# A two-layer backbone on one core: TensorE's attention instructions pinned to written order, transposes and values two steps behind the scores

## The chip, the cores and the metric

The kernel runs on one NeuronCore of a Trainium2 chip. The metric is the device time of one execution in microseconds (us). The core's engines work side by side, each through a queue of its own that it takes in order: TensorE (PE) does matrix products and writes them to PSUM, VectorE (DVE) and ScalarE (ACT) do elementwise work and empty PSUM, GpSimd (POOL) does a few small vector operations, and SyncE (SP) issues the transfers from memory (DMA).

## The reference, cut to what matters

Two streams of 256 tokens ("lat" and "ctx", 1024 features) go through two layers: attention and a feed-forward block, then a state-space mixer and a feed-forward block. The change lies in layer 0's attention alone:

```
q, k, v = split(u @ w_in)                 # 16 query heads, 4 key/value heads of 64
qr, kr  = rope(q_lat), rope(k_lat)        # rotated in the lat stream
s_win   = qr . kr * scale, masked to |i - j| <= 128
s_ctx   = q . k_ctx * scale
p       = softmax([s_win, s_ctx, sink])
y_lat   = (p_win @ v_lat + p_ctx @ v_ctx) @ w_out
# ctx queries attend to ctx keys alone
m       = silu(c) @ w_mod[i] + b_mod[i]   # six modulation vectors of each layer
```

All is float32. Large products split each operand in a high part that TensorE multiplies as fp32r and a low part (the rest), and add three products: high by high, low by high, high by low.

## The kernel before

A framework builds the program. The kernel's author writes Python that emits instructions; tiles come from pools with a number of buffers for each tag; a list scheduler then orders every engine's instructions by its own model of when operands are ready. So the order on TensorE is not the order in the text, unless an instruction is pinned behind its predecessor.

Attention works in 8 **pairs** p of query heads and 3 **steps** t of each pair. Steps 0 and 1 are the two blocks of 128 lat queries (512 keys), step 2 is both blocks of ctx queries (256 keys each). A step goes through these stages:

- `scores(p, t)`: TensorE writes two PSUM banks `s` (one for each head, a = 0 and 1), in fp32r with 128x128 weights, with a bf16 product for the mask in steps 0 and 1. VectorE takes the maxima (two reductions), three small operations make the bias, ScalarE takes the exponentials into `P` (two for each step, four in step 2) and one for the sink, VectorE adds, inverts and scales `P`.
- `mix(p, t)`: eight float32 transposes `pt` of 128x128 (TensorE), two copies to `PT` (ScalarE), then the values `o`: float32 products with 64 columns of weights, the two heads in the two column halves of the array. In steps 0 and 1 that is 8 instructions of 128 columns, in step 2 it is 4 of 256. ScalarE and VectorE split the sum into `oh` and `ol`.
- `q_gemm(p)`: 24 fp32r products of 512 columns for one pair's queries (`q`), copied to `qf`; `q_parts(p)` splits and rotates them (VectorE and ScalarE) into `qe`, `qo`, `re`, `ro`. `emit_w` splits every weight tile into `wh` (ScalarE) and `wl` (VectorE).
- the **filler**: `mods` computes three blocks of layer 0's modulation, each of 8 loads `wm` of 512 KB and 4 float32 products for each (`mod`, 32 columns of weights, the four in the four column quarters), then two transposes and two additions.

The text of `attention` runs the mix of a step one step behind its scores, a query product after the scores of t = 1, and one filler piece a step (two at t = 1). `kv_start` runs before attention, the output product `ao` behind it. PSUM has 8 banks: 4 of tag `mm` (scores, q), 3 of `aux` (pt, o), one `md` (mod). SP's queue holds the loads of `wm` (two buffers) and of raw weights `raw` (two buffers), in order.

In the profile a matrix instruction of float32 stands as two records, one of fp32r, bf16 or of a transpose as one.

Of the kernel before, what the change touches and what calls it, by code (L numbers as in the profile page):

```python
# [39 lines left out]
class Net:  # L40
# [33 lines left out]

    def gemm(self, ps, w, ah, al, c0, c1, ks=range(8)):
        mm = self.nc.tensor.matmul
# [13 lines left out]
    def mods_mm(self, ps, k, wm):  # L90
        n = wm.shape[1] // 4
        for j in range(4):
            self.nc.tensor.matmul(ps[32 * j:32 * j + 32, 0:n], self.cs[:, k, :], wm[:, j * n:(j + 1) * n],
                                  start=(k == 0), stop=(k == 7))

    def mods_out(self, i, ps, n, cuts, streams=(0, 1)):

        nc = self.nc
        m4 = self.tmp.tile([128, 256], F32, tag="t1", name="m4")[:, :n]
        nc.scalar.copy(m4, ps[:, 0:n])  # L100
        q = n // 128
        pt = ps[:, 256:512]
        for c in range(q):
            nc.tensor.transpose(pt[:, c * 128:(c + 1) * 128], m4[:, c * 128:(c + 1) * 128], self.ident)
# [58 lines left out]
    def run(self, gen):  # L163
        for _ in gen:
            pass

# [277 lines left out]
    def scores(self, p, t, q):  # L444
        nc = self.nc
        mm = nc.tensor.matmul
        qe, qo, re, ro = q
        g = p // 2
        P = [self.ap.tile([128, 512], F32, tag="P", name=f"P{p}{t}{a}", bufs=4) for a in range(2)]
# [43 lines left out]
    def mix(self, p, t, P):  # L493
        nc = self.nc
        g = p // 2
        PT = [self.ap.tile([128, 512], F32, tag="PT", name=f"PT{p}{t}{a}", bufs=3) for a in range(2)]
        for a in range(2):
            pt = self.bank("aux", f"pt{p}{t}{a}")
            for c in range(4):

                o = c if t < 2 else 2 * (c % 2) + c // 2
                nc.tensor.transpose(pt[:, o * 128:o * 128 + 128], P[a][:, c * 128:c * 128 + 128], self.ident)
            nc.scalar.copy(PT[a], pt)
        n, keys = (128, range(4)) if t < 2 else (256, range(2, 4))
        po = self.bank("aux", f"o{p}{t}")[:, :n]
        for i, kt in enumerate(keys):
            for a in range(2):
                nc.tensor.matmul(po[64 * a:64 * a + 64, :], self.V[:, kt, g * 64:g * 64 + 64],  # L508
                                 PT[a][:, i * n:i * n + n], start=(i == 0), stop=(i == len(keys) - 1))
# [26 lines left out]
    def kv_start(self, uh, ul):  # L536
# [17 lines left out]
        self.qs = {}  # L554
        for h in range(4):
# [4 lines left out]
            for t in range(4):  # L560
# [4 lines left out]
                if h == 3 and t == 1:  # L565
                    self.qs[0] = self.q_parts(0, q0)
# [15 lines left out]
    def attention(self, uh, ul, filler, k0, kr, k1, q1):  # L582
        qs = self.qs
        pend = []
        for p in range(8):
            q = qs.pop(p)
            for t in range(3):
                P = self.scores(p, t, q)
                pend.append((p, t, P))
                if p == 0 and t == 0:  # L590
                    qf = self.q_gemm(2, uh, ul, "aux")
                    self.k_parts(1, k0, kr)
                    kr = self.k_rope(k1)
                    qs[1] = self.q_parts(1, q1)
                if p == 0 and t == 1:
# [12 lines left out]

    def q_gemm(self, p, uh, ul, tag):
        w = self.next_w()  # L610
        ps = self.bank(tag, f"q{p}")
        self.gemm(ps, w, uh, ul, 0, 512)
        qf = self.ap.tile([128, 512], F32, tag="qf", name=f"qf{p}", bufs=1)
        self.nc.scalar.copy(qf, ps)
        return qf

    def q_parts(self, p, ps):
        qe = self.aq.tile([128, 512], F32R, tag="qe", name=f"qe{p}", bufs=3)
        qo = self.aq.tile([128, 512], F32R, tag="qo", name=f"qo{p}", bufs=3)
        re = self.aq.tile([128, 256], F32R, tag="re", name=f"re{p}", bufs=3)  # L620
        ro = self.aq.tile([128, 256], F32R, tag="ro", name=f"ro{p}", bufs=3)
        self.qsplit(qe, qo, ps)
        qr = self.aq.tile([128, 256], F32, tag="kr", name=f"qr{p}")
        self.rope(qr, ps[:, 0:256])
        self.qsplit(re, ro, qr)
        return qe, qo, re, ro


    def setup(self, ctx):
        tc, nc, a = self.tc, self.nc, self.a  # L630
        self.ctx = ctx
        pool = lambda n, b, **k: ctx.enter_context(tc.tile_pool(name=n, bufs=b, **k))
# [541 lines left out]
```

## Time and profile before

| | us |
|---|---|
| median of 3 runs (lowest to highest) | 1193.76 (1191.71 to 1194.17) |
| the profiled execution | 1194.7 |
| its span in the trace | 1192.9 |
| TensorE busy | 1140.3 (96%) |
| VectorE busy | 839.5 (70%) |
| ScalarE busy | 604.3 (51%) |
| DMA, mean over the span | 153 GB/s |

1.8 us of the profiled execution lie outside its span. A busy TensorE is an engine that has an instruction in flight; the ends of its instructions are modelled and overlap, so what its instructions cost is read from start to start. Positions below are us from the start of the span. Attention takes from 64.3 (the first product of pair 2's queries) to 220.5 (the last product of the values).

### The profile page before, as it was taken

What the parts mean: (1) busy time and instruction counts of PE and PEld (TensorE: products, weight loads), DVE (VectorE), ACT (ScalarE), POOL (GpSimd) and SP (SyncE); (2) the same over time, 40 slices, a digit from 0 to 9 for tenths busy, and PEclk for the clock granted to TensorE, in tenths of its full rate; (3) what the DMA queues carried; (4) which work ended last, traced back from release to release, by engine and by line L of the source; (5) the groups of instructions that cost most, each with busy time, mean ns of one, the idle gap of its engine ahead of it and who ended that gap; (6) DMA issues with size and microseconds to landing.
All of it is one profiled execution on the core that took longest, in us unless ns stands there. A gap on an engine that the chain in (4) does not pass through costs nothing.

```text
span 1192.9 us, 18539 instructions
## 1 busy us (share of the span) xinstructions
PE 1140.3 (96%) x6976; PEld 917.5 (77%) x6976; DVE 839.5 (70%) x1701; ACT 604.3 (51%) x1382; POOL 48.1 (4%) x79
## 2 busy tenths in 40 slices
PE   5999999998999999999999999999999996999996
PEld 4766666887987878887898777777777575898895
DVE  4498677677967677763434879889898769565566
ACT  4376566325532322321422737687868857454551
POOL 1200000003100000000000310000000000000000
PEclk8999999999999999999999989999999998999999
DMA  8834322342445466762222124443545572555551
GB/s 323 305 106 156 128 85 94 91 157 72 159 160 182 157 226 207 249 215 92 85 71 87 64 107 128 131 153 129 189 142 155 186 242 83 200 177 182 202 181 71
DMA packets 41433, 182.79 MB, mean 153 GB/s; under 512 B 4608, under 2 KB 5248, under 8 KB 28288
## 3 DMA queue, kind: packets, MB, share of 16 engines
q1 hardware_dynamic: 41056, 181.36, 45.1%
q8 instruction: 55, 0.90, 0.3%
q10 hardware_dynamic: 288, 0.26, 0.1%
q14 instruction: 34, 0.28, 0.1%
HBM read 180.41 MB, written 1.18 MB: 152 GB/s over the span
## 4 chain that ended last, share of the span: by engine, by line
PE 79%; DVE 8%; DMA 5%; ACT 5%; issue 1%; DVEq 0%; SPq 0%; ACTq 0%
PE f0a L79 5%; PE f0a L80 5%; PE f0a L81 5%; PE f0b L79 5%; PE f0b L81 5%; PE f0b L80 5%; PE y L947 3%; PE o L508 2%; PE f L265 2%; PE f L264 2%; PE f L263 2%; PE f1a L81 2%; PE f1a L79 2%; PE f1a L80 2%; DMA raw<-in_wall 2%; PE x L81 2%
## 5 line engine op out<-in xcount | busy, mean ns | idle before, releaser
L61 ACT CAST wh<-raw 128x512 fp32r<-128x512 f32 x404 | 237.6, 619 | 400.5 <-PE f0b L80 126.3
L62 DVE TENSOR_TENSOR wl<-raw,wh 128x512 fp32r<-128x512 f32 x404 | 268.4, 686 | 129.3 <-ACT wh L61 128.4
L79 PE MATMUL f0b<-f0fh,wh 128*128 128x512 f32 (+1 forms) x320 | 113.8, 356 | 0.0
L79 PE MATMUL f0a<-u1h,wh 128*128 128x512 f32 (+1 forms) x320 | 112.2, 353 | 1.5 <-ACT u1h L183 1.5
L81 PE MATMUL f0b<-f0fh,wl 128*128 128x512 f32 (+1 forms) x320 | 111.9, 350 | 0.0
L80 PE MATMUL f0a<-u1l,wh 128*128 128x512 f32 (+1 forms) x320 | 111.4, 350 | 0.0
L81 PE MATMUL f0a<-u1h,wl 128*128 128x512 f32 (+1 forms) x320 | 111.4, 349 | 0.0
L80 PE MATMUL f0b<-f0fl,wh 128*128 128x512 f32 (+1 forms) x320 | 111.1, 347 | 0.1
L142 DVE SCALAR_TENSOR_TENSOR ma<-wm,cs,ma 128x1024 f32<-128x1024 f32 x70 | 88.7, 1280 | 17.8 <-DMA wm<-in_w_mod 17.7
L79 PEld LDWEIGHTS f0a<-u1h,wh 128*128 128x128 f32 x320 | 61.1, 192 | 11.8 <-ACT u1h L183 2.3
L81 PEld LDWEIGHTS f0b<-f0fh,wl 128*128 128x128 f32 x320 | 60.1, 188 | 10.4 <-issue 2.1
L79 PEld LDWEIGHTS f0b<-f0fh,wh 128*128 128x128 f32 x320 | 60.1, 188 | 10.4 <-issue 2.6
L80 PEld LDWEIGHTS f0b<-f0fl,wh 128*128 128x128 f32 x320 | 60.2, 188 | 9.7 <-issue 1.4
L81 PEld LDWEIGHTS f0a<-u1h,wl 128*128 128x128 f32 x320 | 61.2, 191 | 8.0 <-issue 0.4
L80 PEld LDWEIGHTS f0a<-u1l,wh 128*128 128x128 f32 x320 | 61.0, 191 | 7.7 <-issue 0.4
L79 PE MATMUL f1a<-u4h,wh 128*128 128x256 f32 x224 | 63.5, 284 | 0.0
L81 PE MATMUL f1a<-u4h,wl 128*128 128x256 f32 x224 | 63.5, 283 | 0.0
L80 PE MATMUL f1a<-u4l,wh 128*128 128x256 f32 x224 | 63.4, 283 | 0.0
L79 PE MATMUL x<-u2h,wh 128*128 128x512 f32 x128 | 51.5, 402 | 2.2 <-DVE cy L758 2.2
L931 ACT ACTIVATE W<-A,sT 128x128 f32<-128x128 f32 (+1 forms) x128 | 50.0, 458 | 3.8 <-PE y L947 2.5
L351 DVE SCALAR_TENSOR_TENSOR X<-f0b,mT,X 128x256 f32<-128x256 f32 x48 | 21.0, 478 | 44.0 <-PE f0b L81 44.0
L81 PE MATMUL x<-u2h,wl 128*128 128x512 f32 x128 | 51.3, 402 | 0.3 <-DVE wl L62 0.3
(439 smaller groups left out, 2747.3 us busy)
## 6 DMA issues: line engine op xcount, KB each, us to landing
raw<-in_wall SPq DMA_DIRECT2D x102, 1024.0 KB, 5.0
wm<-in_w_mod SPq DMA_DIRECT2D x96, 512.0 KB, 4.3
A<-dq SPq DMA_DIRECT2D x32, 256.0 KB, 4.7
E<-dq SPq DMA_DIRECT2D x32, 256.0 KB, 5.0
X<-in_xT SPq DMA_DIRECT2D x8, 256.0 KB, 8.1
gate<-in_rows SPq DMA_DIRECT2D x2, 512.0 KB, 12.9
out_dram<-Xt SPq DMA_DIRECT2D x4, 256.0 KB, 2.0
mixg<-in_rows SPq DMA_DIRECT2D x1, 512.0 KB, 6.1
```

The costliest lines, as they stand in the source:

```text
L61: nc.scalar.copy(h, src[:, c])
L62: nc.vector.tensor_sub(l, src[:, c], h.bitcast(F32))
L79: mm(ps, wh[:, k, :], ah[k][:, c0:c1], start=(k == 0), stop=False)
L80: mm(ps, wh[:, k, :], al[k][:, c0:c1], start=False, stop=False)
L81: mm(ps, wl[:, k, :], ah[k][:, c0:c1], start=False, stop=(k == 7))
L142: nc.vector.scalar_tensor_tensor(t, wm, c, t, op0=ALU.mult, op1=ALU.add)
L263: mm(ps, lh(i), wh[:, c], start=(k == 0), stop=False)
L264: mm(ps, ll(i), wh[:, c], start=False, stop=False)
L265: mm(ps, lh(i), wl[:, c], start=False, stop=last)
L508: nc.tensor.matmul(po[64 * a:64 * a + 64, :], self.V[:, kt, g * 64:g * 64 + 64], PT[a][:, i * n:i * n + n], start=(i == 0), stop=(i == len ...
L931: nc.scalar.activation(W[:, h, o:o + l1 - l0], A[:, h, l0:l1], AF.Relu, scale=-1.0, bias=self.sT[:, st, r + h:r + h + 1])
L947: mm(ps[64 * a:64 * a + 64, l0:l1], lh[:, hc:hc + 64], mv, start=(n == 0), stop=(n == 5))
```

## The change

`pin(True)` makes `self.mm` and `self.tr` wrap every TensorE product and transpose traced in attention, the filler's and the query products' too, in `keep_in_program_order`: an edge of order behind the instruction written before on TensorE. The other engines and SP stay with the scheduler. `mix` is cut into `turn` (transposes and copies) and `mix` (values). One step now writes, in this order: the transposes of the step two behind, the scores of its own, a third of a query product (9, 9 and 6 instructions of 24), a filler piece, the values of the step two behind. The products for pair 2 and pair 3 stand whole ahead of and behind the first scores. The filler gives one piece a step in pairs 0 to 5 and two in pairs 6 and 7. Buffers: `P` 4 to 6, `PT` 3 to 4, `qf` 1 to 2, `qe`, `qo`, `re`, `ro` 3 to 2. All engines have the same instructions in the same number; before attention's first query product and behind its last values the order is the same on every engine.

```
+    def pin(self, on):
+        if on:
+            self.mm = lambda *a, **k: self.tc.keep_in_program_order(self.nc.tensor.matmul(*a, **k))
+            self.tr = lambda *a, **k: self.tc.keep_in_program_order(self.nc.tensor.transpose(*a, **k))
+        else:
+            self.mm, self.tr = self.nc.tensor.matmul, self.nc.tensor.transpose
...
     def attention(self, uh, ul, filler, k0, kr, k1, q1):
         qs = self.qs
-        pend = []
+        late, parts = [], []
+        self.pin(True)
+        qg = self.q_gemm(2, uh, ul, "mm", 1)
+        self.run(qg)
         for p in range(8):
+            for _ in self.chain(*parts):
+                pass
             q = qs.pop(p)
             for t in range(3):
-                P = self.scores(p, t, q)
-                pend.append((p, t, P))
+                old = late.pop(0) if len(late) > 1 else None
+                if old is not None:
+                    PT = self.turn(*old)
+                late.append((p, t, self.scores(p, t, q)))
                 if p == 0 and t == 0:
-                    qf = self.q_gemm(2, uh, ul, "aux")
+                    self.run(self.q_parts(1, q1))
+                    self.run(self.q_gemm(3, uh, ul, "aux", 1))
+                if p == 0 and t == 1:
                     self.k_parts(1, k0, kr)
...
-                for _ in range(1 + (t == 1)):
+                for g in parts:
+                    next(g, None)
+                if t == 1 and 0 < p < 5:
+                    qg = self.q_gemm(p + 3, uh, ul, "mm", 3)
+                next(qg, None)
+                for _ in range(1 if p < 6 else 2):
                     next(filler, None)
-                if len(pend) > 1:
-                    self.mix(*pend.pop(0))
-                if t == 0 and p < 6:
-                    qs[p + 2] = self.q_parts(p + 2, qf)
-                if t == 1 and p < 5:
-                    qf = self.q_gemm(p + 3, uh, ul, "mm")
-        while pend:
-            self.mix(*pend.pop(0))
+                if old is not None:
+                    self.mix(*old[:2], PT)
+            parts = []
+            if p < 6:
+                parts = [self.q_parts(p + 2, self.qfs.pop(p + 2))]
+        for old in late:
+            self.mix(*old[:2], self.turn(*old))
+        self.pin(False)
```

In the rows of order below a name's first digits are the pair, the step and the head (`s401` is pair 4, step 0, head 1; `o31` are the values of pair 3, step 1; `mod04` is the third block of the filler, `wm042` its load for piece 2).

On TensorE, at the first step of pair 4, before:

```order
L459 MATMUL s401_1725<-krh_140,ro4_1311 128x256
L508 MATMUL o31_1704<-PT310_1690,V_144 64x128
L460 MATMUL s401_1725<-krl_141,ro4_1311 128x256
L461 LDWEIGHTS identb_98
L461 MATMUL s401_1725<-maskb_99,identb_98 128x128
L464 MATMUL s401_1725<-kph_142,qo4_1309 128x256
L508 MATMUL o31_1704<-PT311_1691,V_144 64x128
```

The same step now (the wrapped instructions have the line of `pin`):

```order
L78 MATMUL s401_1682<-kpl_143,qo4_1415 128x256
L78 MATMUL q6_1548<-u0h6_107,wh10_1093 128x512
L78 MATMUL q6_1548<-u0l6_115,wh10_1093 128x512
L78 MATMUL q6_1548<-u0h6_107,wl10_1094 128x512
L78 MATMUL q6_1548<-u0h7_108,wh10_1093 128x512
L78 MATMUL q6_1548<-u0l7_116,wh10_1093 128x512
L78 MATMUL q6_1548<-u0h7_108,wl10_1094 128x512
L78 MATMUL mod03_1481<-wm033_1707,cs_81 32x256 x4
L78 MATMUL o31_1713<-PT310_1658,V_144 64x128
L78 MATMUL o31_1713<-PT311_1659,V_144 64x128
```

The values of a step stood between the scores in two pieces, and now stand whole behind the scores, the query products and the filler's piece.

On VectorE, where the maxima of pair 0's second step (`st01`) are taken, before:

```order
L466 TENSOR_REDUCE st01_852<-s010_853 128x1
L441 TENSOR_TENSOR re1_809<-qr1_815,re1_809 64x256
L442 TENSOR_TENSOR ro1_810<-qr1_815,ro1_810 64x256
L423 STREAM_SHUFFLE rt_841<-qf2_791 128x256
L422 TENSOR_TENSOR qr2_840<-qf2_791,con0_100 128x256
L424 TENSOR_TENSOR rt_841<-rt_841,con0_100 128x256
L466 TENSOR_REDUCE st01_852<-s011_860 128x1
```

The same place now:

```order
L62 TENSOR_TENSOR wl10_1094<-raw10_1091,wh10_1093 128x512
L476 TENSOR_REDUCE st01_853<-s010_854 128x1
L476 TENSOR_REDUCE st01_853<-s011_861 128x1
L435 TENSOR_TENSOR kr_886<-kr_886,rt_887 128x256
L486 TENSOR_TENSOR st01_853<-st01_853,sink8_145 128x2
L444 TENSOR_TENSOR kpl_143<-kq2_308,kph_142 64x256
L487 TENSOR_SCALAR st01_853<-st01_853 128x2
```

Most of the splitting and rotating of pair 2's queries left this stretch for pair 1, and the two maxima stand together, among the keys' splits.

On TensorE, where the third block's third and fourth filler pieces stand, before (pair 5, steps 0 and 1):

```order
L93 MATMUL mod04_1820<-wm042_1972,cs_81 32x256 x4
L459 MATMUL s510_2020<-krh_140,re5_1540 128x256
L460 MATMUL s510_2020<-krl_141,re5_1540 128x256
L461 LDWEIGHTS identb_98
L461 MATMUL s510_2020<-maskb_99,identb_98 128x128
L464 MATMUL s510_2020<-kph_142,qe5_1538 128x256
L465 MATMUL s510_2020<-kpl_143,qe5_1538 128x256
L93 MATMUL mod04_1820<-wm043_2044,cs_81 32x256
```

The same pieces now (pair 6, step 1):

```order
L78 MATMUL s611_2168<-kph_142,qo6_1864 128x256
L78 MATMUL s611_2168<-kpl_143,qo6_1864 128x256
L78 MATMUL mod04_2120<-wm042_2185,cs_81 32x256 x4
L78 MATMUL mod04_2120<-wm043_2191,cs_81 32x256 x4
L78 MATMUL o52_2197<-PT520_2144,V_144 64x256
L78 MATMUL o52_2197<-PT521_2145,V_144 64x256
```

The third block moved back by a pair, and its pieces come two at a time, which is as many as `wm` has buffers.

## Rows read from the trace of the kernel before

**Rows 1.** Stretches: us, PE, PEld, DVE, ACT, POOL busy, clock, DMA share, GB/s

```profile
68.00:111.40 43.40, 40.06 (x273) 28.20 (x272) 37.59 (x105) 27.65 (x73) 0.00 (x0) 0.96 0.45 151
111.40:131.30 19.90, 19.84 (x144) 13.94 (x142) 13.88 (x46) 12.78 (x36) 0.00 (x0) 1.00 0.27 81
131.30:152.20 20.90, 20.84 (x152) 14.22 (x150) 13.96 (x44) 12.61 (x36) 0.00 (x0) 1.00 0.45 152
152.20:172.50 20.30, 19.52 (x146) 13.88 (x144) 14.07 (x46) 12.96 (x37) 0.00 (x0) 1.00 0.27 78
172.50:186.90 14.40, 13.97 (x120) 8.91 (x117) 12.33 (x43) 9.91 (x32) 0.00 (x0) 1.00 0.67 220
...
186.90:209.80 22.90, 22.57 (x184) 16.54 (x181) 16.30 (x59) 15.10 (x50) 1.00 (x6) 1.00 0.09 24
```

**Rows 2.** Timeline of TensorE: start, us to the last end, line, names, records

```profile
155.97 0.39 PE L459 MATMUL s<-krh,re 128*128 128x256 f32 x1
157.27 0.38 PE L104 MATMUL mod<-con,m 128*128 128x128 f32 x2
...
191.26 0.28 PE L460 MATMUL s<-krl,ro 128*128 128x256 f32 x1
191.47 1.09 PE L508 MATMUL o<-PT,V 128*64 128x128 f32 x14
192.49 1.09 PE L502 MATMUL pt<-con,P 128*128 128x128 f32 x8
...
193.64 0.28 PE L465 MATMUL s<-kpl,qo 128*128 128x256 f32 x1
193.85 0.64 PE L93 MATMUL mod<-wm,cs 128*32 128x256 f32 x8
...
194.65 0.28 PE L471 MATMUL s<-kpl,qe 128*128 128x256 f32 x1
194.76 0.29 PE L470 MATMUL s<-kph,qe 128*128 128x256 f32 x1
```

**Rows 3.** The same view: a filler piece between values, query products, four sets of filler

```profile
91.39 1.06 PE L93 MATMUL mod<-wm,cs 128*32 128x256 f32 x14
...
164.66 0.64 PE L93 MATMUL mod<-wm,cs 128*32 128x256 f32 x8
165.23 1.09 PE L508 MATMUL o<-PT,V 128*64 128x128 f32 x14
...
166.58 0.39 PE L79 MATMUL q<-u0h,wh 128*128 128x512 f32 x1
166.81 0.39 PE L80 MATMUL q<-u0l,wh 128*128 128x512 f32 x1
```

**Rows 4.** VectorE's groups in attention: line, names, count, busy us, mean ns, idle before

```profile
L489 DVE TENSOR_SCALAR P<-P,st 128x512 f32<-128x512 f32 (+1 forms) x64 | 23.2, 416 | 0.4
L466 DVE TENSOR_REDUCE st<-s 128x1 f32<-128x512 f32 x32 | 21.8, 686 | 2.5 <-PE s L465 2.1
L62 DVE TENSOR_TENSOR wl<-raw,wh 128x512 fp32r<-128x512 f32 x18 | 12.1, 684 | 10.2 <-ACT wh L61 10.1
L486 DVE RECIPROCAL st<-st 128x2 f32<-128x2 f32 (+1 forms) x24 | 3.9, 162 | 0.1
L424 DVE TENSOR_TENSOR rt<-rt,con 128x256 f32<-128x256 f32 x9 | 3.8, 420 | 0.0
```

**Rows 5.** Timeline of TensorE: transposes that waited for `P`

```profile
75.17 1.09 PE L502 MATMUL pt<-con,P 128*128 128x128 f32 x8 [1.01 <-DVE P L489]
```

**Rows 6.** Timeline of VectorE: the softmax of pair 3's last step

```profile
150.97 1.28 DVE L472 TENSOR_REDUCE st<-s 128x2 f32<-128x512 f32 x2
...
157.87 1.14 DVE L489 TENSOR_SCALAR P<-P,st 128x256 f32<-128x256 f32 x4
```

**Rows 7.** The tile `wm` in attention and after: its loads

```profile
DMA to landing us min/median/max: 3.4/3.8/6.8
```

**Rows 8.** A stretch of pair 1, columns as in rows 1

```profile
94.00:100.00 6.00, 5.47 (x22) 3.81 (x21) 5.97 (x21) 2.83 (x10) 0.00 (x0) 0.72 0.53 193
```

More of the change, by code (lines that the diff above doesn't have):

```diff
@@ L92, in mods_mm @@
         for j in range(4):
-            self.nc.tensor.matmul(ps[32 * j:32 * j + 32, 0:n], self.cs[:, k, :], wm[:, j * n:(j + 1) * n],
-                                  start=(k == 0), stop=(k == 7))
+            self.mm(ps[32 * j:32 * j + 32, 0:n], self.cs[:, k, :], wm[:, j * n:(j + 1) * n],
+                    start=(k == 0), stop=(k == 7))
     def mods_out(self, i, ps, n, cuts, streams=(0, 1)):
@@ L103, in mods_out @@
         for c in range(q):
-            nc.tensor.transpose(pt[:, c * 128:(c + 1) * 128], m4[:, c * 128:(c + 1) * 128], self.ident)
+            self.tr(pt[:, c * 128:(c + 1) * 128], m4[:, c * 128:(c + 1) * 128], self.ident)
         ptv = pt[:, :n].rearrange("p (c j r) -> p j c r", c=q, j=4)
@@ L163, in run @@
     def run(self, gen):
-        for _ in gen:
+        last = None
+        for last in gen:
             pass
+        return last
     def affine(self, name, gv, bv, streams, scale, shift):
@@ L445, in scores @@
         nc = self.nc
-        mm = nc.tensor.matmul
+        mm = self.mm
         qe, qo, re, ro = q
         g = p // 2
-        P = [self.ap.tile([128, 512], F32, tag="P", name=f"P{p}{t}{a}", bufs=4) for a in range(2)]
+        P = [self.ap.tile([128, 512], F32, tag="P", name=f"P{p}{t}{a}", bufs=6) for a in range(2)]
         T = 1 if t < 2 else 2
@@ L491, in scores, with turn @@
         return P
-    def mix(self, p, t, P):
+    def turn(self, p, t, P):
         nc = self.nc
-        g = p // 2
-        PT = [self.ap.tile([128, 512], F32, tag="PT", name=f"PT{p}{t}{a}", bufs=3) for a in range(2)]
+        PT = [self.ap.tile([128, 512], F32, tag="PT", name=f"PT{p}{t}{a}", bufs=4) for a in range(2)]
         for a in range(2):
@@ L501, in mix @@
                 o = c if t < 2 else 2 * (c % 2) + c // 2
-                nc.tensor.transpose(pt[:, o * 128:o * 128 + 128], P[a][:, c * 128:c * 128 + 128], self.ident)
+                self.tr(pt[:, o * 128:o * 128 + 128], P[a][:, c * 128:c * 128 + 128], self.ident)
             nc.scalar.copy(PT[a], pt)
+        return PT
+    def mix(self, p, t, PT):
+        nc = self.nc
+        g = p // 2
         n, keys = (128, range(4)) if t < 2 else (256, range(2, 4))
@@ L507, in mix @@
             for a in range(2):
[L508 to L509 removed]
+                self.mm(po[64 * a:64 * a + 64, :], self.V[:, kt, g * 64:g * 64 + 64],
+                        PT[a][:, i * n:i * n + n], start=(i == 0), stop=(i == len(keys) - 1))
         c = slice(t * 128, t * 128 + n)
@@ L565, in kv_start @@
                 if h == 3 and t == 1:
-                    self.qs[0] = self.q_parts(0, q0)
+                    self.run(self.q_parts(0, q0))
             self.v_gemm(vb, vs, uh, ul, range(2 * h, 2 * h + 2))
@@ L613, in q_gemm @@
-        qf = self.ap.tile([128, 512], F32, tag="qf", name=f"qf{p}", bufs=1)
-        self.nc.scalar.copy(qf, ps)
-        return qf
-    def q_parts(self, p, ps):
[L618 to L621, printed above, removed]
+        cut = [0, 8] if parts == 1 else [0, 3, 6, 8]
@@ new lines, in q_gemm @@
+        for n in range(parts):
+            self.gemm(ps, w, uh, ul, 0, 512, range(cut[n], cut[n + 1]))
+            if n == parts - 1:
+                qf = self.qfs[p] = self.ap.tile([128, 512], F32, tag="qf", name=f"qf{p}")
+                self.nc.scalar.copy(qf, ps)
+            yield self.qfs.get(p)
+    def q_parts(self, p, ps):
+        qe = self.aq.tile([128, 512], F32R, tag="qe", name=f"qe{p}", bufs=2)
+        qo = self.aq.tile([128, 512], F32R, tag="qo", name=f"qo{p}", bufs=2)
+        re = self.aq.tile([128, 256], F32R, tag="re", name=f"re{p}", bufs=2)
+        ro = self.aq.tile([128, 256], F32R, tag="ro", name=f"ro{p}", bufs=2)
+        self.qs[p] = (qe, qo, re, ro)
```

14 lines of the change are left out of this document (7 added, 7 removed).

## The prediction

> **What bounds the kernel now.** I first cut attention into stretches at the first score products of pairs 2, 3, 4, 5 and 6 (111.4, 131.3, 152.2, 172.5, 186.9) and at the end of the last scores (209.8), and read each engine's busy time in them [rows 1]. TensorE is busy 19.84 of 19.90 us in pair 2, and nearly so in pairs 3 and 4: it sets the pace there, and VectorE works 14 us of each 20. Up to 111.4 it is otherwise: VectorE's busy time of 37.59 in 43.40 counts overlaps once, and the sum of its instructions' own durations, counted below in the same way, is 42.4, so it is full, and TensorE waits for it [rows 5]. In one stretch of pair 1 it is busy 5.97 of 6.00 [rows 8].
>
> Next I asked what a busy TensorE spends its time on, and read its timeline from start to start. Inside a run of one kind the prices are steady: a query product 0.23 (166.58 to 166.81) [rows 3], a score product 0.11 (194.65 to 194.76), a transpose 0.11 (eight in 1.09 to the end of the last, less the last one's own 0.3), a step's ten score products 1.30 (155.97 to 157.27) [rows 2]. A filler piece is two sets of four products, 0.21 a set: four sets take 1.06 where two take 0.64 [rows 3]. Two values side by side take 0.11 (14 records in 1.09) [rows 2, 3].
>
> With these a pair with a query product holds 24 x 0.23 = 5.5 (queries), 2 x 1.30 + 8 x 0.11 = 3.5 (scores), 24 x 0.11 = 2.6 (transposes), 24 x 0.11 = 2.6 (values; a value of 256 columns counts as two), and 4 x 0.43 = 1.7 (filler): 15.9 us. Pairs 2 to 4 took 61.1, or 20.4 each [rows 1]. The missing 4.5 us sit at the changes of kind. From a score product to filler there are 0.21 (193.64 to 193.85) in place of 0.11. From a score product to values there are 0.21 too, and from the 14 records' start to the transposes 1.02 in place of 0.76 [rows 2]. The scheduler cut most values in two and put them between scores and queries, so these changes come often; from transposes to scores I find none to pay.
>
> **The change, part by part.** No instruction is added or removed. The order on TensorE changes, and with it that of VectorE, ScalarE and the loads.
>
> *Fewer changes of kind.* A step is now transposes, scores, queries, filler, values. It pays scores to filler 0.10, filler to values 0.57 - 0.43 = 0.14 (164.66 to 165.23) [rows 3], and values to transposes 1.02 - 0.76 = 0.26 [rows 2]: 0.50 a step. With three filler pieces a pair holds 15.5, so pairs 2 to 4 take 3 x (15.5 + 1.5) + 0.2 (two more transposes of the filler's end) = 51.2 in place of 61.1: **-9.9**. Bounds: 48 if the changes cost nothing, 61 if in-order waiting returns all of it; I take the priced value, because VectorE's orders for these three pairs sum to 46 and so still fit under it.
>
> The first of those prices meets a rule. The Trainium skill (TensorEngine Tiling, Key Properties) says that a change of the tiling mode, not only of the tile, drains TensorE; filler uses quarter columns and values half, so by the rule their meeting is a full change too. Were it to cost the 0.24 that a change costs on average between scores and values, 24 steps would pay 2.4 us more and the sum would be 1184.4. The row shows 0.14, and the sum keeps it.
>
> *Start.* TensorE now stands in order behind the transposes of the step two behind, so its first scores of pair 2 come when VectorE has scaled `P` of pair 1's second step. VectorE's order lists until there, from 68.0 on: 11 maxima x 0.69, 10 scalings x 0.42, 6 halves of `wl` x 0.68, 4 splits the size of such a half, 32 operations of 256 columns x 0.42, 25 small ones x 0.16 and 3 `ol` of 0.3 [rows 4]: 7.6 + 4.2 + 4.1 + 2.7 + 13.4 + 4.0 + 0.9 = 36.9. That gives 104.9, plus one block of transposes, 0.9: 105.8 in place of 111.4, **-5.6**. The splits of pair 3's queries no longer stand all ahead of it. Bounds: -5.6 (full, as VectorE was) and 0 (each step waits for ScalarE).
>
> *Pair 5.* TensorE reaches the transposes of this pair's second step after 11.9 us of its own. VectorE's order holds 15.3 us by the same prices until that `P` is scaled: 6 maxima, the scalings of three steps, the rotation and half of the splits of pair 7's queries, two halves of `wl`, some twenty small operations. It begins 0.8 behind the first scores, so pair 6 begins after 0.8 + 15.3 + 0.9 = 17.0 in place of 14.4 [rows 1]: **+2.6**. Bounds: 13.3 (TensorE's own) and 18.
>
> *Pairs 6 and 7.* The filler's third block now comes here, two pieces a step. TensorE's own work until the last scores end is 7.0 (scores), 3.6 (filler), 4.4 (values), 4.4 (transposes) and 5 x 0.5: 21.9 in place of the 22.9 us that the stretch took [rows 1]. But `wm` has two buffers, both freed by the two pieces, and the next two loads have the values, transposes and scores of a step to land: 1.1 + 0.9 + 1.3 = 3.3 us. Loads took 3.4 to 6.8, median 3.8 [rows 7]. The second of two asked for together lands later, so I charge 1.0 three times: 24.9, **+2.0** (0 to +10). On SP the raw weights' loads moved ahead of some `wm`; a raw buffer is freed by `wl`, which stands ahead of the `wm` it would hold up, so nothing is charged.
>
> *End.* Behind the last scores the same chain is left (10.7 us, the rest to 220.5), less one block of transposes, which now stands ahead: **-0.9**. Behind that the order is the old one on every engine, and I carry the shift to the end.
>
> Sum: -9.9 - 5.6 + 2.6 + 2.0 - 0.9 = -11.8. The profiled execution took 1194.7, so 1182.9; the median of the runs lies 0.9 lower, so **1182.0**.
>
> **The rivals.** *TensorE alone binds.* VectorE's 15.3 us in pair 5 overlap better and loads land in time: pair 5 gives 13.3 - 14.4 = -1.1, pairs 6 and 7 give -1.0. Sum -18.5: 1175.3. For it: VectorE has 5 us to spare in pairs 2 to 4; against: its order is fixed, so it can't use them for pair 5.
>
> *VectorE and ScalarE bind throughout.* VectorE waited 10.2 us for `wh` alone [rows 4]; if it waits half a microsecond a step in the dense order, pairs 2 to 4 take 18.7 each and give -5, the start gives -3, the others stay: -4 to -6, some 1189. Against it: VectorE's 46 us for these pairs leave 5 spare.
>
> *Slower: the softmax outlasts two steps.* TensorE reaches the transposes of a step 9.9 us behind its scores: twice queries 2.1, filler 0.5 and values 1.3, once transposes 0.9 and scores 1.3. The softmax of pair 3's last step took from 150.97 to 159.0 on VectorE, 8.0 [rows 6]. What exceeds 9.9 is paid half in each step, and everything on TensorE stands behind it, scores of the next step included, while before the scheduler had other products ahead of it. The point is 11.2 us: 18 steps (pairs 2 to 7) x 0.66 eat the 11.8. At 13 us it is 18 x 1.55 = 28 against 11.8: 1211. For it: transposes waited 1.01 where VectorE was full [rows 5]; against: the slack of 1.9 in pairs 2 to 4. The Trainium skill (TensorE: Matmul & The Clock Gate, Step-by-step) says that only weight loads are pulled ahead and products keep their order, which is what makes a waiting transpose hold up all the rest; the 1.01 us in which TensorE had nothing else agree.
>
> *It doesn't do what it says.* If each block of filler and of values costs its price wherever it stands (0.42 and 0.45, from scores to scores), 24 steps pay 0.87 in place of 0.50, 9 us more, of which the waits in pairs 0, 1 and 5 hide some 3: 1188. Against it is the 0.14 between filler and values.
>
> A smaller cost for all: in one stretch of pair 1 the granted clock averaged 0.72, part of it at 1.2 in place of 2.4 GHz, after TensorE had waited [rows 8], 6 x 0.28 = 1.7 us. The new waits of pairs 0 and 1 may bring one or two such stretches; VectorE's lead there hides most of it.
>
> **How the numbers follow.** Chances: forecast 0.55 (1178 to 1187), TensorE alone 0.15, VectorE and ScalarE 0.17, slower 0.09, not what it says 0.04. The predicted time is the first one's. The range runs from 1176 to 1191: it cuts off most of the TensorE case's lower end, the slower case and the top of the VectorE case. A difference of 0.2%, 2.4 us, is about what a measurement here can tell from none; so faster is 0.55 + 0.15 + 0.12 + 0.04 = 0.86, same 0.05, slower 0.09.
>
> **What would show it.** The filler's and values' records stand in whole blocks, once a step, with about 0.14 between them; pair 2's first scores begin near 106, pair 5's near 157, pair 6's near 174, and the last values end near 209. TensorE waits for `P` in pairs 0, 1 and 5 and hardly in 2 to 4, and for `wm` in pairs 6 and 7. VectorE has less idle time. If pairs 2 to 4 take over 18.5 each with TensorE waiting for `P` or `PT`, the slower or the VectorE case holds; if they take 17 but blocks cost more than 0.5 a step, a price is wrong.

## The result and the profile after

| | before | after |
|---|---|---|
| median, us (lowest to highest, 4 runs each) | 1192.74 (1191.45 to 1194.17) | 1178.55 (1177.08 to 1180.05) |
| the profiled execution | 1194.7 | 1180.05 |
| its span | 1192.9 | 1178.3 |

The ratio is 0.9879, with a 95% interval of 0.9863 to 0.9895: 14.2 us faster, where 11.8 were predicted. TensorE was busy 1120.6 us in place of 1140.3, with the same 6976 instructions.

The stretches, from the first query product on and cut at the first score products of pairs 2 to 7 (columns as in [rows 1]):

```profile
62.80:105.30 42.50, 38.11 (x267) 29.07 (x265) 40.09 (x114) 29.68 (x77) 0.00 (x0) 0.92 0.44 139
105.30:121.60 16.30, 16.30 (x136) 12.70 (x134) 14.46 (x45) 12.97 (x41) 0.00 (x0) 1.00 0.29 92
121.60:138.20 16.60, 16.60 (x142) 12.56 (x141) 13.64 (x43) 11.86 (x36) 0.00 (x0) 1.00 0.43 135
138.20:154.90 16.70, 16.70 (x144) 12.66 (x142) 13.59 (x43) 12.22 (x37) 0.00 (x0) 1.00 0.34 95
154.90:169.10 14.20, 12.23 (x119) 9.46 (x117) 12.32 (x44) 12.02 (x39) 0.00 (x0) 1.00 0.52 178
169.10:183.90 14.80, 13.15 (x143) 9.24 (x141) 11.15 (x37) 10.75 (x32) 0.00 (x0) 1.00 0.58 182
```

Pairs 2 to 4 take 16.3 to 16.7 us each in place of 20 to 20.9, and TensorE has no idle time in them. What each stretch gained or lost, between the same products in both traces:

| stretch | before | after | change | predicted |
|---|---|---|---|---|
| to pair 2's first scores (position) | 111.38 | 105.28 | -6.1 | -5.6 |
| pairs 2 to 4 | 61.1 | 49.6 | -11.5 | -9.9 |
| pair 5 | 14.4 | 14.2 | -0.2 | +2.6 |
| pairs 6, 7, to the last score product | 22.65 | 24.7 | +2.1 | +2.0 |
| from there to the end of the last values | 11.3 | 9.6 | -1.7 | -0.9 |
| attention in all | | | -17.4 | -11.8 |
| behind attention | | | +2.8 | 0 |

Of the first row, 1.8 us lie ahead of the changed part: the first product of pair 2's queries comes at 62.5 in place of 64.3, and at 64.6 in a second profile of the changed kernel. From that product on, attention is 15.6 us shorter.

The waits of TensorE in attention and its output product (what waited, for what: us in total, times, longest) and, from its timeline, one step of pair 3, the wait for `P` in pair 5 and one wait in pair 6:

```profile
PE pt L79 <- DVE P L499: 4.0, 2, 2.1
PE mod L78 <- DMA wm<-in_w_mod: 2.7, 3, 1.1
PE s L78 <- ACT P L492: 1.7, 1, 1.7
PE aosum L206 <- DVE X L346: 1.5, 2, 1.3
```

```profile
129.89 0.39 PE L78 MATMUL q<-u0h,wl 128*128 128x512 f32 x1
130.21 0.64 PE L78 MATMUL mod<-wm,cs 128*32 128x256 f32 x8
130.78 1.08 PE L78 MATMUL o<-PT,V 128*64 128x256 f32 x8
131.79 1.09 PE L79 MATMUL pt<-con,P 128*128 128x128 f32 x8
...
168.21 1.11 PE L79 MATMUL pt<-con,P 128*128 128x128 f32 x8 [1.97 <-DVE P L499]
...
181.45 0.64 PE L78 MATMUL mod<-wm,cs 128*32 128x256 f32 x8 [1.12 <-DMA wm<-in_w_mod]
```

Filler and values stand in whole blocks, once a step. From filler to values there are 0.57 us in place of the 0.43 of a filler piece alone, so the 0.14 of [rows 3] again.

### The profile page after: what moved, and what is told of

Its sections match the earlier page's. It is cut to its first block, busy times and chain, and to the rows that moved or that the text cites. A ratio compares the mean times of both kernels' runs of the same rounds, so it can differ in the third digit from the quotient of the medians.

```text
span 1178.3 us, 18541 instructions
## 1 busy us (share of the span) xinstructions
PE 1120.6 (95%) x6976; PEld 911.6 (77%) x6976; DVE 838.2 (71%) x1701; ACT 603.3 (51%) x1382; POOL 48.2 (4%) x79
## 4 chain that ended last, share of the span: by engine, by line
PE 80%; DVE 8%; DMA 6%; ACT 5%; issue 1%; SPq 0%; DVEq 0%; ACTq 0%
PE f0a L87 5%; PE f0a L88 5%; PE f0a L89 5%; PE f0b L87 5%; PE f0b L89 5%; PE f0b L88 5%; PE y L983 3%; PE f L275 2%; PE f L274 2%; PE f L273 2%; PE f1a L89 2%; PE f1a L87 2%; PE f1a L88 2%; PE q L78 2%; DMA wm<-in_w_mod 2%; PE x L89 2%
## 5 line engine op out<-in xcount | busy, mean ns | idle before, releaser
L87 PEld LDWEIGHTS f0a<-u1h,wh 128*128 128x128 f32 x320 | 61.6, 193 | 11.8 <-ACT u1h L193 2.3
## 6 DMA issues: line engine op xcount, KB each, us to landing
gate<-in_rows SPq DMA_DIRECT2D x2, 512.0 KB, 12.8
```

## The experiments

All kernels compute everything. Those of one group ran on one chip beside the kernel before; the changed kernel itself, run again, gave 1178.93 us, a ratio of 0.9896 (0.9881 to 0.9911). Against its two ratios, 0.9879 and 0.9896, I hold the others. In the order on TensorE I also counted how often it goes from one kind (scores and queries; transposes; filler; values) to another in pairs 2 to 4: 72 times before, 36 after.

**The price of a change of kind.** In the query product a third is cut again, and the step's values stand in two halves around the cut:

```
-            self.gemm(ps, w, uh, ul, 0, 512, range(cut[n], cut[n + 1]))
+            self.gemm(ps, w, uh, ul, 0, 512, range(cut[n], cut[n + 1] - (parts > 1)))
+            if parts > 1:
+                yield None
+                self.gemm(ps, w, uh, ul, 0, 512, range(cut[n + 1] - 1, cut[n + 1]))
...
-                    self.mix(*old[:2], PT)
+                    m = self.mix(*old[:2], PT)
+                    next(m)
+                    next(qg, None)
+                    next(m, None)
```

> Nothing is computed otherwise. In twelve steps of pairs 1 to 5 (nine of them in pairs 2 to 4) the step's values are cut into two halves with three of the step's query products between them, which stood ahead of the filler; so each of these steps has one more change from query products to values and back. Theory (the gain of the change in pairs 2 to 4 is the price of changes of kind, and TensorE sets the pace there): a meeting with values costs what the rows of before and after give, 0.43 to 0.48 us for going to them and back, so pairs 2 to 4 take 49.6 + 9 x 0.48 = 53.9 us and the whole kernel 4.3 to 5.7 us more than the changed kernel, about 1183.5. Rival (TensorE has slack there, the gain came from waits that the written order removed): the halves hide in idle time, 0 to 1 us more.

Measured: 1183.22 us, 0.9931 (0.9919 to 0.9944). Pairs 2 to 4, then a step of pair 3:

```profile
105.10:122.50 17.40, 17.40 (x136) 12.33 (x135) 14.53 (x47) 14.18 (x46) 0.00 (x0) 1.00 0.22 67
122.50:140.20 17.70, 17.70 (x142) 12.20 (x141) 13.88 (x42) 12.01 (x33) 0.00 (x0) 1.00 0.44 145
140.20:158.00 17.80, 17.80 (x144) 12.30 (x142) 14.14 (x43) 12.41 (x39) 0.00 (x0) 1.00 0.31 92
```

```profile
125.14 0.66 PE L78 MATMUL o<-PT,V 128*64 128x128 f32 x8
125.73 0.50 PE L78 MATMUL q<-u0h,wh 128*128 128x512 f32 x1
...
126.62 0.66 PE L78 MATMUL o<-PT,V 128*64 128x128 f32 x8
127.21 1.09 PE L79 MATMUL pt<-con,P 128*128 128x128 f32 x8
```

The same work, busy to the last tenth, takes 52.9 us in place of 49.6: 3.3 us for nine meetings, 0.37 each. It can be seen in the step: from the first query product to the second values there are 0.89 us for three products of 0.23, 0.20 too much, and from the first half's start to the query product 0.59 for values of 0.43, 0.16 too much. So a meeting costs TensorE time where nothing makes it wait, and the theory holds; its 0.43 to 0.48 was some 20% high, since it took the 0.26 of the prediction for leaving the values (the second half leaves for the transposes after 0.59 too). The rest of what the kernel lost lies elsewhere: pairs 6 and 7 took 26.8 us in place of 24.7, at a granted clock of 0.94 and with 0.5 us more of waits for `wm`, and the end of attention 10.7 in place of 9.6.

**The written order alone.** One line is taken out:

```
-        self.pin(True)
```

> The same program text without the rule that TensorE keeps the written order: the scheduler may move its instructions again. In pairs 2 to 5 it gives the written order all the same; in pairs 0 and 1 it puts values, filler and scores of neighbouring steps among each other, and in pairs 6 and 7 it mixes scores, transposes and filler. Theory (cutting the query products into three parts and taking transposes and values two steps behind is what makes the gain in pairs 2 to 4): these pairs take 49.6 us again, within 0.5, and the time differs from the changed kernel's only by what the ends do, -3 to +4 us. Rival (holding TensorE to the written order is itself what gains): pairs 2 to 4 go back toward 61 us and the time to 1188 or more.

Measured: 1175.71 us, 0.9863 (0.9848 to 0.9878), the 3 us at the edge of what the intervals tell apart. Pairs 2 to 4 and the start:

```profile
67.70:103.00 35.30, 33.42 (x250) 23.47 (x249) 33.36 (x99) 24.14 (x65) 0.00 (x0) 1.00 0.44 141
103.00:120.30 17.30, 17.19 (x129) 13.11 (x127) 15.73 (x50) 14.20 (x43) 0.00 (x0) 1.00 0.29 92
120.30:136.90 16.60, 16.60 (x142) 12.57 (x141) 13.69 (x43) 11.82 (x36) 0.00 (x0) 1.00 0.44 136
136.90:153.60 16.70, 16.70 (x144) 12.67 (x142) 13.59 (x43) 12.05 (x36) 0.00 (x0) 1.00 0.32 96
```

The gain in pairs 3 and 4 is there to the tenth; in pair 2 the scheduler cuts two steps' values in two, which takes 0.9 us more, and the pair begins 2.3 us earlier than in the changed kernel. So holding TensorE to the written order gains nothing here: what gains is in the rest of the new text (the cut, the distance, the filler's place, transposes apart from values). With the pin TensorE stands behind waits at the ends that the scheduler's order steps past: of the 4.0 us for `P` and 2.7 us for `wm`, 0.4 and none are left.

**Two steps behind, alone.** The kernel before, with one edit (and two more buffers for `P`):

```
-                if len(pend) > 1:
+                if len(pend) > 2:
```

> The kernel before with one edit: transposes and values two steps behind the scores in place of one (six buffers for P in place of four); the scheduler may still move TensorE's instructions, query products are not cut. It still cuts nearly all values in two and puts them among scores and query products: 64 changes of kind in pairs 2 to 4 in place of 72. Theory (the price of changes): eight fewer at about 0.2 us, 1.6 us, so pairs 2 to 4 take 59.5 in place of 61.1 and the time is 0 to 3 us under the kernel before, 1189 to 1192. Rival (the distance of two steps makes the gain, since the softmax no longer holds TensorE up): most of the 11.5 us of pairs 2 to 4, 1180 to 1183.

Measured: 1187.02 us, 0.9946 (0.9933 to 0.996).

```profile
65.90:105.10 39.20, 36.82 (x255) 25.72 (x255) 37.23 (x104) 26.97 (x71) 0.00 (x0) 1.00 0.46 150
105.10:124.70 19.60, 19.60 (x145) 14.09 (x143) 14.88 (x47) 12.70 (x36) 0.00 (x0) 1.00 0.34 128
124.70:144.40 19.70, 19.63 (x150) 14.05 (x149) 13.87 (x44) 12.45 (x36) 0.00 (x0) 1.00 0.48 161
144.40:163.20 18.80, 18.80 (x146) 13.78 (x144) 14.06 (x46) 12.83 (x37) 0.00 (x0) 1.00 0.29 85
```

Pairs 2 to 4 take 58.1 us, 3.0 less for 8 changes of kind less; 0.8 of it is idle time that went, so some 2.2 are left for the changes. The rival's distance doesn't make the gain in these pairs, and the theory's 1.6 is near. The whole kernel was faster than the 1189 to 1192 expected, for what I had not expected is the start: pair 2 begins at 105.1 here too, 39.2 us behind the first scores in place of 44.4. So the distance of two steps, with its two buffers, shortens the start without pin and without cut.

**The cut of the query products, alone.** The changed kernel, with the products in one piece:

```
-                    qg = self.q_gemm(p + 3, uh, ul, "mm", 3)
+                    qg = self.q_gemm(p + 3, uh, ul, "mm", 1)
```

> The changed kernel with the query products of a pair not cut in three: all 24 stand in the pair's middle step, as in the kernel before; TensorE still keeps the written order, and transposes and values are two steps behind. TensorE changes its kind 36 times in pairs 2 to 4, as often as in the changed kernel (72 times in the kernel before). Theory (prices of changes, and a slot in which the softmax must fit): the sum stays, but the slot behind the scores of each pair's last step has no query product, 5.8 us in place of 9.9. With one step behind the slot was 3.9 and TensorE waited 2.25 us a step, so the softmax needed about 6.2 to 6.5 there, and up to 8.0 where VectorE is loaded: 0.4 to 2.2 us for each of the four or five pairs that follow query products, so +2 to +11 us on the changed kernel, about 1184, with waits of transposes for P. Rival (the cut itself makes the gain, by shorter runs between the softmax steps, whatever the waits): pairs 2 to 4 go back toward 61 us, 1188 to 1190. Third (the cut does nothing): within 1 us.

Measured: 1182.25 us, 0.9909 (0.9896 to 0.9923). Pairs 2 to 4 take 52.7 us, 3.1 more than with the cut and 8.4 less than before, and 2.0 of the 3.1 are waits: with 36 changes of kind the price theory holds without the cut. The slot theory has its size but not its place. TensorE waited 1.2 us for `P` once, in pair 2; in the pairs behind it, the steps without query products wait for the copies `PT`:

```profile
142.99 0.43 PE L78 MATMUL o<-PT,V 128*64 128x128 f32 x2
144.11 1.09 PE L78 MATMUL o<-PT,V 128*64 128x128 f32 x14 [0.69 <-ACT PT L513]
```

ScalarE's timeline shows why: the first copy runs at once, the second stands behind four exponentials.

```profile
140.95 0.59 ACT L513 COPY PT<-pt 128x512 f32<-128x512 f32 x1 [0.37 <-PE pt L79]
141.56 0.47 ACT L492 ACTIVATE P<-s,st 128x256 f32<-128x256 f32 x1
...
143.47 0.59 ACT L513 COPY PT<-pt 128x512 f32<-128x512 f32 x1
```

**What a fixed order costs when it waits.** Transposes right ahead of their values, still two steps behind:

```
-                if old is not None:
-                    PT = self.turn(*old)
...
-                    self.mix(*old[:2], PT)
+                    self.mix(*old[:2], self.turn(*old))
```

> Nothing is computed otherwise. The transposes of a step no longer stand ahead of the next scores but right ahead of their own values, at the same distance of two steps. Theory (a wait of TensorE in its fixed order is paid in full): each step's values wait for ScalarE's copy of the transposed weights, which before the change stood between them. From the last transpose to the copy's end is about 1.2 us, and one change of kind falls away (0.26), so about 0.9 us a step, 21 to 23 steps: +19 to +26 us, some 1200. Rival (such waits hide in TensorE's slack or in VectorE's lead, as much of the start does): 0 to 5 us more.

Measured: 1213.53 us, 1.018 (1.0165 to 1.0194), 35 us more than the changed kernel. And transposes and values one step behind:

```
-                old = late.pop(0) if len(late) > 1 else None
+                old = late.pop(0) if len(late) > 0 else None
```

> Nothing is computed otherwise. Transposes and values stand one step behind the scores in place of two. Theory of the slower rival (what the softmax needs beyond the slot is paid by TensorE in each step): the slot from a step's scores to its transposes is then one step's queries, filler and values, 3.9 us (1.9 in pairs 6 and 7), while the chain of maximum, exponentials and scaling took 6.5 to 8.0; 2.6 to 4 us a step over 23 steps give +60 to +90 us, 1240 to 1270. If TensorE were held by something else in most steps (VectorE's list in pairs 0, 1 and 5, the loads in pairs 6 and 7), only pairs 2 to 4 would pay, 9 x 2.6 to 4 = +23 to +36, 1202 to 1215. Rival (the distance doesn't matter because the cut alone makes the gain): within 2 us of the changed kernel.

Measured: 1231.69 us, 1.0332 (1.0313 to 1.0351), 53 more. The waits of TensorE (first joined, then one step behind), each with a stretch of its pairs (pair 3 of the first, pair 4 of the second):

```profile
PE o L78 <- ACT PT L513: 20.4, 22, 2.2
```

```profile
130.80:154.40 23.60, 20.21 (x141) 14.45 (x140) 14.99 (x43) 12.48 (x35) 0.00 (x0) 0.93 0.35 113
```

```profile
PE pt L79 <- DVE P L499: 50.9, 22, 5.2
```

```profile
164.80:188.40 23.60, 18.19 (x142) 13.79 (x141) 14.71 (x43) 12.48 (x36) 0.00 (x0) 0.93 0.23 67
```

The rival, that such waits hide, falls in both. Both prices were off. Joined, 0.9 us a step were expected and pairs 2 to 4 took 2.3 a step more. Half of that is idle time, 10.7 of 20.6 us, since ScalarE doesn't copy at once: with TensorE's transposes at 125.21, its copies began at 127.79, behind four exponentials that came first in its order. The clock, 0.94 on average there, makes some 4 us more by my estimate, and the other 6 I have not taken apart. One step behind, 2.6 to 4 us a step were expected and 2.25 were paid, 1.8 of it idle; the slot of 3.9 and these 1.8 make 5.7 us for the softmax, less than the 6.5 to 8.0 I had taken, and why it needs less no run shows. The granted clock was 0.93 in the two stretches shown, where it was 1.00 in the changed kernel: for a part of them TensorE ran at 1.2 in place of 2.4 GHz.

**The waits for `wm` in pairs 6 and 7.** Two ways to take them away: the filler's old cadence, and a third buffer.

```
-                for _ in range(1 if p < 6 else 2):
+                for _ in range(1 + (t == 1)):
```

> The filler goes back to the cadence of the kernel before: two pieces in the middle step of each pair and one in the others, to the end of its three blocks, in place of one a step and two in pairs 6 and 7. Pairs 1 to 5 then hold one more piece each (0.4 us) and pairs 6 and 7 fewer. Theory (the 2.7 us that TensorE waits for the loads of wm in pairs 6 and 7 stand on the path): these waits go, the pieces cost the same wherever they stand, and the time falls by 2.0 to 2.7 us, to about 1176. Where the doubled pieces now make TensorE wait for a load in pairs 1 to 5, it would show there as a wait for the DMA of wm, up to 1 us a pair. Rival (behind attention the sum of the modulations waits for DMA anyway, so time won in pairs 6 and 7 is given back there): 0, within 0.7 us.

Measured: 1178.74 us, 0.9893 (0.9879 to 0.9906), no difference. Pairs 6 and 7 took 21.6 us, 3.2 less, but pairs 2 to 5 took 66.9 in place of 63.8, and the start 38.4 in place of 37.3. Neither the theory's sum nor the rival came out: the gain was not given back behind attention but never got out of it. The waits had moved to where the doubled pieces now stood, which the expectation had named as an exception, and they are longer there, three of 3.9 us in all in place of 2.7; and pairs 1 to 5 held a piece more each.

```
-        P = [self.ap.tile([128, 512], F32, tag="P", name=f"P{p}{t}{a}", bufs=6) for a in range(2)]
+        P = [self.ap.tile([128, 512], F32, tag="P", name=f"P{p}{t}{a}", bufs=5) for a in range(2)]
...
-        with tc.tile_pool(name="wm", bufs=2) as self.wm:
+        with tc.tile_pool(name="wm", bufs=3) as self.wm:
```

> Three buffers for wm in place of two, and five for P in place of six to make room. The order on TensorE stays. Theory (the loads of wm, which wait for a buffer, hold up TensorE in pairs 6 and 7 and the sum of the modulations behind attention): the 2.7 us of waits go and some of the 2.8 us that were given back behind attention too: -2.5 to -5 us, 1174 to 1176. Rival (loads are held up elsewhere, by their queue, or the end of attention has its own bound): 0 to -1. If five P buffers are too few, scores wait for the bank of P: up to +1 us a pair in pairs 0 to 2.

Measured: 1175.31 us, 0.9865 (0.985 to 0.988), 3.6 us less than the changed kernel on the same chip. No wait for `wm` is left in attention, pairs 6 and 7 took 21.65 us, 3.1 less, and the sums behind `ao` began 3.4 us earlier. The waits stood on the path.

**VectorE's list at the start.** The lower parts of the rotated keys of groups 1 to 3 are taken on GpSimd:

```
+        eng = nc.gpsimd if pool else nc.vector
...
-            nc.vector.tensor_sub(lo[64 * b:64 * b + 64, g, :], src, hi[64 * a:64 * a + 64, g, :].bitcast(F32))
+            eng.tensor_sub(lo[64 * b:64 * b + 64, g, :], src, hi[64 * a:64 * a + 64, g, :].bitcast(F32))
...
-        self.kdup(self.krh, self.krl, g, kr[c, :])
+        self.kdup(self.krh, self.krl, g, kr[c, :], g > 0)
```

> The six subtractions that make the lower parts of the rotated keys of groups 1 to 3 (64 partitions x 256 columns) go to GpSimd in place of VectorE; nothing else is moved. They stand in VectorE's list of 36.9 us ahead of pair 2. Theory (VectorE is full at the start and its list sets when pair 2 begins): six operations of 0.42 us leave the list, so pair 2's first scores come 2 to 2.5 us earlier (near 103) and the time falls by as much, to about 1176.5. Rival (the start hangs on the chain of ScalarE and VectorE, step by step, not on VectorE's sum): 0 to -0.7 us. If GpSimd's slower operation holds up the scores of pairs 2 to 6, that shows as a wait of scores for GpSimd.

Measured: 1177.89 us, 0.9889 (0.9872 to 0.9906): the time is within its error of the changed kernel's. The place is clearer than the time. From the first scores to pair 2, in the changed kernel run again and here:

```profile
70.10:106.80 36.70, 31.19 (x243) 23.74 (x242) 35.22 (x105) 24.98 (x67) 0.00 (x0) 0.95 0.44 139
```

```profile
68.40:103.30 34.90, 29.80 (x244) 22.39 (x242) 32.62 (x98) 25.53 (x71) 3.61 (x5) 1.00 0.46 146
```

The stretch is 1.8 us shorter and VectorE has 2.6 us less to do, which looks like the theory. But TensorE's idle time fell by 0.4 us only, from 5.5 to 5.1, and its busy time by 1.4, at a clock of 1.00 in place of 0.95. And VectorE's list does not set when pair 2 begins: its last `P` ahead of pair 2 was scaled at 103.43 and taken by TensorE at 105.95 in the changed kernel, at 97.46 and 102.44 here. So the theory's path is not shown; most of the gain came with the clock, and why that was higher no run here shows. On GpSimd one of the six operations took 0.73 us, on VectorE 0.42. The Trainium skill (GPSIMD Engine Reference, Engine selection) says to leave operations of two inputs to VectorE since GpSimd takes about twice as long; the factor is 1.7 here. That the move is worth it all the same is not shown, for the time didn't move beyond its error.

**Together.** Both edits that won, first with the written order, then without:

> The changed kernel with the two edits that won, together: three buffers for wm (five for P), and the six subtractions of the rotated keys' lower parts on GpSimd. They bear on different places (pairs 6 and 7; the start), so theory says that they add: 3.6 us and 1.0 to 2.4 us, 1173 to 1174.5. Rival (what the start gains is waited for at the loads behind attention, as 2.8 us of the change itself were): 1175.3, no better than the buffers alone.

> The two edits that won (three buffers for wm, the six subtractions on GpSimd) and TensorE's order left to the scheduler, which gives the written order in pairs 2 to 5 all the same and moves instructions only in pairs 0, 1, 6 and 7. Theory (the written order costs at the ends, where TensorE stands behind waits for P and wm that it could step past): the free order gained 3.0 us by itself, of which the third wm buffer gains the same waits in pairs 6 and 7 again; what is left to it is pairs 0 and 1, 1 to 2 us: 1171.5 to 1174. Rival (the free order cuts more values in two in pairs 6 and 7 and pays 0.37 us for each meeting): no better than the pinned form with both edits, 1173 to 1175.5.

Measured: 1173.63 us, 0.9843 (0.9822 to 0.9863), with the written order, and 1172.79, 0.9834 (0.982 to 0.9848), without. Both are faster than the changed kernel by some 5 us. That fits edits that add, but the first one's interval overlaps that of the buffers alone (0.985 to 0.988), so only the buffers' gain is clear of noise. Between the two orders the intervals don't decide. Without the pin the stretch from the first scores to pair 2 is 1.7 us shorter (33.2 against 34.9) and pairs 2 to 4 take 0.4 more. Pairs 5 to 7 take 37.1 in both, with the pin at a clock of 0.95; the pinned kernel with the buffers alone took 35.8 there at 1.00. So with the third buffer I see nothing that the free order gains in these pairs.

## Why the prediction was right, step by step

**What bounds** was read rightly in pairs 2 to 4 (TensorE, by its changes of kind and not by waits) and in pair 5 (VectorE's list). At the start it was not. And the total came out better than its terms: pairs 2 to 4, pair 5, the start and the end gave 1.6, 2.8, 0.5 and 0.8 us more than forecast, and 2.8 us lost behind attention, where nothing was charged, took half of that back. That the errors partly cancel is luck.

**Fewer changes of kind** (-9.9, measured -11.5). The mechanism held. The price of one change was mis-sized, from values to transposes, 0.26 us in the sum and 0.15 in the trace after:

```profile
187.55 1.09 PE L78 MATMUL o<-PT,V 128*64 128x128 f32 x16
188.58 1.09 PE L79 MATMUL pt<-con,P 128*128 128x128 f32 x8
```

A whole block of 16 records, eight turns of two heads side by side at 0.11 each, takes 1.03 to the transposes. The forecast found the same 1.02 behind 14 records in [rows 2] and read them as seven turns. But there one product (two records) of one head had been cut off, and the four of the other head still take eight turns. So a cut costs a turn beside its changes, and the change itself less. A step's changes come to 0.38 us by the starts (0.09 from queries to filler, 0.14, 0.15) and not to 0.50, which is 1.1 of the 1.6 us. Another 0.4 is a filler piece: these pairs hold eight and not nine, the ninth turn being the filler's transposes. And not all of the 11.5 us are changes of kind: 0.9 was idle time before, and two filler pieces (0.9) went to other pairs.

The runs with 36, 54, 64 and 72 changes, at 49.6, 52.9, 58.1 and 61.1 us, stand in that order; the uncut one has 36 too, and most of what it takes beyond 49.6 are waits. What the forecast had wrong is the tool: it gave the whole blocks to the written order, and with the rest of the new text the free order has them too. Which part of that text makes the scheduler keep the blocks no run shows.

By the Trainium skill (TensorEngine Tiling, Key Properties) a change of tiling mode drains TensorE, and the prediction said what the sum would be if the change between filler and values cost a full 0.24. The trace after shows 0.14 again, and the measured time lies on the row's side of the sum. No run here contradicts the rule itself: every change to or from values or filler costs something, some 0.1 to 0.2 us in these rows, by what meets what.

**Start** (-5.6, measured -6.1). The number came out by luck; the mechanism failed. The sum had TensorE's transposes of pair 1's second step wait for VectorE's list. TensorE's last wait for `P` in the start and these transposes, then VectorE's scaling of that `P`:

```profile
91.18 1.24 PE L79 MATMUL pt<-con,P 128*128 128x128 f32 x8 [2.05 <-DVE P L499]
...
104.44 1.09 PE L79 MATMUL pt<-con,P 128*128 128x128 f32 x8
```

```profile
101.03 0.87 DVE L499 TENSOR_SCALAR P<-P,st 128x512 f32<-128x512 f32 x2
```

```profile
91.18:105.28 14.10, 14.10 (x100) 10.74 (x101) 13.19 (x42) 8.89 (x24) 0.00 (x0) 0.88 0.37 121
```

The `P` was ready at 101.9, and TensorE came to it 2.5 us later without a wait. Behind its wait for pair 0's last step, at 91.18, it is busy for all 14.10 us, at a clock of 0.88: so its own work ended last, and the smaller cost that the prediction named, stretches at half clock, is in it. VectorE's list itself took 33.5 us (68.4 to 101.9). Its durations sum to 36.8, as forecast, but they overlap by 5.0, and VectorE was idle for 1.7. Nor was VectorE full before, as the prediction had it up to 111.4:

```profile
100.00:106.00 6.00, 6.00 (x46) 3.92 (x46) 3.62 (x11) 4.18 (x12) 0.00 (x0) 1.00 0.30 87
```

What the start gained from is known in part: 1.8 us lie ahead of it; six query products and two filler pieces (2.2 us by the forecast's prices) stand behind pair 2's first scores now; and the stretch has 21 changes of kind in place of 32, at a lower clock, 0.92 in place of 0.96. How the gain divides among these and the distance of two steps no run separates.

**Pair 5** (+2.6, measured -0.2): the term that failed. Its mechanism is there, TensorE waits 1.97 us at 168.21 for the `P` that VectorE scales last. The size is not: the list took 12.8 us (155.75 to 168.55), not 15.3. The step that failed is the price of an operation by its duration, since operations that need nothing of their predecessor start before its recorded end. VectorE's timeline:

```profile
156.35 0.15 DVE L495 TENSOR_TENSOR st<-st 128x4 f32<-128x4 f32 x1
156.42 0.28 DVE L527 TENSOR_TENSOR ol<-o,oh 128x128 fp32r<-128x128 f32 x1
156.62 0.17 DVE L496 RECIPROCAL st<-st 128x4 f32<-128x4 f32 x1
156.71 0.66 DVE L476 TENSOR_REDUCE st<-s 128x1 f32<-128x512 f32 x1
157.29 1.13 DVE L499 TENSOR_SCALAR P<-P,st 128x256 f32<-128x256 f32 x4
```

The first four take 0.94 from start to start where their durations sum to 1.26. Over the list the durations sum to the forecast's 15.3 us, the overlap is 3.0 and the idle time 0.5. The same overlap was in the start's sum.

**Pairs 6 and 7** (+2.0, measured +2.1): three waits for `wm` of 0.5, 1.1 and 1.1 where three of 1.0 were taken. The third buffer took them away, and 3.1 us with them.

**End** (-0.9, measured -1.7) was somewhat short; why, no run shows.

**Behind attention** (0, measured +2.8): this step failed too. The forecast put it at nothing because the order is the old one there, but the loads are not done earlier for it. VectorE's sums `ma` waited 2.9 us for the loads `wm`, 1.5 before, and the sums of `ao` waited for VectorE, so 1.2 us were gone at the first product of the feed-forward part. The clock can account for the rest, 1.6: in 60 us that hold the start of the feed-forward products (from 258.0 after, from 274.5 before) the granted clock averaged 0.94, and 0.97 before, which I estimate at 1.8 us.

**The rivals.** In-order waiting was the true danger, as the runs at 1213.5 and 1231.7 show, and two steps were enough to avoid it in pairs 2 to 4. TensorE alone (1175.3) came near in attention, where pair 5 gave -0.2 and not -1.1, and was spoiled by the waits for `wm`.

## What to carry to other kernels

Price what an engine does from start to start, also on VectorE, where independent operations overlapped and a sum of durations came out up to a quarter too high. Before you price a block, count the turns that it takes, and not its records. Where a sum rests on a wait, look for that wait in the trace after: the start's number was right without it. Where an engine is busy all the time, count how often its order changes the shape that it works with, and write the text (shorter pieces, more distance between a producer and its consumer) so that blocks stay whole; then look whether the order has to be fixed at all, for the fixed order paid for its waits here. And where a wait was for a buffer, a third buffer took it away, while moving the work that waited only moved the wait.

## What the runs showed of the hardware

Waits of TensorE cost more than themselves. The run with one step behind was idle 16.1 us in pairs 2 to 4 and took 20.2 more; its granted clock was 0.93 to 0.97 there, 1.00 in the changed kernel, which makes 4.0 us by my estimate, about all of the rest. And behind attention the clock is not the same from kernel to kernel, though TensorE is about as busy (56.9 us of 60); here in the changed kernel, then in the two last ones, with and without the written order:

```profile
258.00:318.00 60.00, 56.90 (x436) 52.46 (x433) 52.44 (x106) 29.53 (x66) 14.88 (x15) 0.94 0.36 116
```

```profile
258.00:318.00 60.00, 56.95 (x431) 51.58 (x431) 54.59 (x103) 29.44 (x66) 11.96 (x11) 1.00 0.42 138
```

```profile
258.00:318.00 60.00, 56.94 (x418) 52.07 (x417) 52.58 (x99) 28.18 (x64) 10.24 (x11) 0.94 0.42 134
```

From the output product's start to the end of the span the last two took 981.0 and 985.6 us. A single profiled execution can thus mislead by some 4 us about a change that ends long before.
